# A convolution's output projection, half of its contraction by seven products and joined to the input projection's loop

## The chip, the core and the metric

The kernel runs on one core of a Trainium2 chip. The metric is the device time of one execution in microseconds (us). A core has five engines with queues of their own: TensorE (PE in the profile; its weight loads are PEld), VectorE (DVE), ScalarE (ACT), GpSimd (POOL) and SyncE (SP), which here only issues DMA transfers. Each engine works through its instructions in a fixed order, and an instruction that waits for a semaphore holds up everything behind it on that engine.

## The reference, cut to what matters

Two layers follow each other, a gated short convolution and a dilated windowed attention, on `x` of 1024 tokens and 1024 channels in float32. The change is in the first layer's end:

```python
h = rms_norm(x, conv_norm)                 # 1024 x 1024
b, c, u, z = split(h @ w_in, 4)            # w_in 1024 x 8192, each part 1024 x 2048
conv = sum(w_conv[k] * shifted(c * u, k) for k in range(3))
y = b * conv * silu(z)                     # 1024 x 2048
x = x + y @ w_out                          # w_out 2048 x 1024: the output projection
h = rms_norm(x, attn_norm)                 # and then the attention layer:
proj = h @ w_in                            # its q, k, v and z projections
```

The normalisation of the second layer needs, for every token, the mean square of the new `x` over all channels.

## The kernel before, in words

Everything is held transposed: channels on the 128 partitions, tokens along the free axis, the 1024 tokens as two halves (`hf` 0 and 1) of 512. A product of two float32 matrices is made from three products of rounded parts: each operand is split into a high and a low part (`split_w` for weights, lines 159 and 160, one ACT and one DVE instruction of 128x512 each; the same pair at lines 532 and 533, or 535 and 536, for activations), and `high*high`, `high*low` and `low*high` are added up in one PSUM bank. `product` (line 296) is the unit: a 512-deep contraction, four 128-deep slices with three matmuls of 128x128 by 128x512 each, so 12 matmuls.

The convolution's input projection and the attention's projection (called the QKV loop here) run in `strassen` (line 314): a pair of output tiles by two token halves and two halves of the contraction would be eight such units; a seven-product scheme makes it with seven, from added and subtracted operands. GpSimd mixes the weights (`mix`, line 274, four instructions a pair), ACT and DVE split them one pair ahead into eight buffers `ws`. The products are numbered 1, 2, 6, 5, 7, 4, 3; 4 and 3 of a pair run inside the next pair. `between(n, at)` hangs other work behind the product at place `at` of pair `n`.

In the input projection the gated result is multiplied together on DVE and GpSimd and stored to DRAM (`ydc`, 16 channel tiles by two halves, line 362). Then comes the output projection: for each token half and each of the eight output tiles `dt`, `chunk` adds four units (q = 0 to 3, 2048 deep) in one bank, plain; `row` adds `x`, stores the new tile to DRAM (`x1d`), splits and scales it into the operand blocks of the QKV loop (`B`, `T`), squares it on ACT and adds the square on GpSimd into `sqacc`. The weights of the output projection are loaded and split once for each half.

From `sqacc` come the statistics. `stats(hf)` sums it over partitions with four small matmuls (line 91) into the one bank of the pool `cst`, and DVE makes the inverse root of it in small instructions on 128x4 elements (lines 97 and 63 to 67, tile `rtok`). `spread(hf, rtok)` transposes `rtok` on PE (line 105) into the same bank, ACT copies it; `spread(hf, ms2)` does the same for the mean squares, and DVE turns them (lines 111, 112). For half 0 all three stand between the rows of half 1 in the output projection, and for half 1 in pair 1 of the QKV loop, at places 0, 5 and 6.

TensorE's order is the program's order (`manual_schedule`). On the other engines a scheduler sets it when the kernel is built. Tiles `f` (12 buffers of 128x512) serve nearly every intermediate. The blocks `blka` to `blkg` and `xb` hold split operands of 512 x 512.

## Time and profile before

| | |
|---|---|
| runs | 1918.7, 1921.18 and 1921.12 us, median 1921.12 |
| the profiled execution | 1914.92 us, of which the span from its first to its last instruction is 1913.1 us |
| busy share of the span | PE 98%, DVE 77%, POOL 48%, ACT 46% |
| input projection | 0 to 636 us of the span |
| output projection | 636 to 812.5 us |
| QKV loop, then attention | from 812.5 us |

The busy time of PE is a modelled one, since matmuls are pipelined: one shows as 0.39 us and the next starts 0.227 us after it. What matters is where PE has nothing to do, and what ends that wait. In the rows of a timeline, the brackets give how long the engine had been idle and who released it.

### The profile page before, as it was taken

Reading aid. Unit: us, or ns where it says so; the run is one execution under the profiler, and the core shown is the slowest. Engines: PE = TensorE matmul, PEld = TensorE weight load, DVE = VectorE, ACT = ScalarE, POOL = GpSimd, SP = SyncE. Lnnn points to the kernel's source line nnn. Section 1 sums busy time; section 2 is a strip of 40 time slices with the busy share of each in tenths; the row PEclk is TensorE's granted clock in tenths of the full one; section 3 lists DMA queues with packets and bytes.
Section 4 is the critical chain, followed back from the end, with each engine's and each line's share of the span. In section 5 each row is a group of like instructions: output and inputs, shape, how many; then the busy total and the mean of one; then the engine's idle time right before and its main releaser. Section 6 shows DMA issues by size and latency. Waiting matters only on the chain. (4 is left out here: it accounts for less than half of the span.)

```text
span 1913.1 us, 30523 instructions
## 1 busy us (share of the span) xinstructions
PE 1881.6 (98%) x10850; PEld 1544.4 (81%) x10850; DVE 1466.4 (77%) x2780; ACT 887.4 (46%) x2037; POOL 911.4 (48%) x841
## 2 busy tenths in 40 slices
PE   8999999999999999999999999999999999989999
PEld 6888888888888788888888888888888886777877
DVE  7966666666656746598988798878888787988886
ACT  6533333333333535454434443433443437978880
POOL 1376666766666211244545554555454562433340
PEclk9999999999999999999999999999999999999999
DMA  6222223222322656423323332433232437896842
GB/s 217 84 81 90 89 76 107 88 88 76 96 83 83 231 164 228 155 94 124 112 89 129 111 115 84 133 107 114 78 132 88 132 123 252 268 303 214 254 130 89
DMA packets 117801, 253.79 MB, mean 133 GB/s; under 512 B 18494, under 2 KB 23838, under 8 KB 117648
## 3 DMA queue, kind: packets, MB, share of 16 engines
q1 hardware_dynamic: 93280, 176.89, 28.4%
q0 software_dynamic: 24368, 74.95, 12.0%
q8 instruction: 85, 1.39, 0.3%
q14 instruction: 68, 0.56, 0.1%
HBM read 192.53 MB, written 67.64 MB: 136 GB/s over the span
## 5 line engine op out<-in xcount | busy, mean ns | idle before, releaser
L160 DVE TENSOR_TENSOR ws<-wr,ws 128x512 fp32r<-128x512 f32 x283 | 287.1, 1017 | 121.1 <-ACT ws L159 119.3
L159 ACT ACTIVATE ws<-wr 128x512 fp32r<-128x512 f32 x283 | 178.0, 630 | 365.2 <-PE pp L302 239.2
L159 ACT ACTIVATE ws<-sr 128x512 fp32r<-128x512 f32 x276 | 173.3, 631 | 342.1 <-PE pp L302 277.7
L274 POOL TENSOR_TENSOR sr<-wr 128x512 f32<-128x512 f32 x138 | 197.5, 1431 | 247.6 <-DMA wr<-in_conv_w_in 106.5
L160 DVE TENSOR_TENSOR ws<-sr,ws 128x512 fp32r<-128x512 f32 x276 | 230.7, 842 | 82.6 <-ACT ws L159 80.4
L311 DVE TENSOR_TENSOR f<-pp,f 128x512 f32<-128x512 f32 x207 | 141.6, 684 | 86.4 <-PE pp L302 79.0
L961 ACT ACTIVATE xs<-xs,nl 128x256 f32<-128x256 f32 (+2 forms) x384 | 160.9, 427 | 0.2 <-DVE nl L955 0.2
L307 ACT ACTIVATE f<-pp 128x512 f32<-128x512 f32 x231 | 134.2, 581 | 6.5 <-PE pp L302 6.5
L274 POOL TENSOR_TENSOR sr<-wr,sr 128x512 f32<-128x512 f32 x69 | 90.5, 1311 | 67.7 <-issue 55.2
L955 DVE CUSTOM_DVE_ANT_0 xs<-ps,bt 128x256 f32<-128x256 f32 (+2 forms) x384 | 102.5, 326 | 19.9 <-PE pt L968 12.2
L299 PE MATMUL pp<-blkf,ws 128*128 128x512 f32 x276 | 109.9, 398 | 0.7 <-ACT f L307 0.7
L299 PE MATMUL pp<-blka,ws 128*128 128x512 f32 x276 | 107.5, 390 | 0.7 <-ACT f L307 0.7
L301 PE MATMUL pp<-blkd,ws 128*128 128x512 f32 x276 | 107.9, 391 | 0.0
L299 PE MATMUL pp<-blkb,ws 128*128 128x512 f32 x276 | 107.8, 390 | 0.0
L299 PE MATMUL pp<-blkd,ws 128*128 128x512 f32 x276 | 107.6, 390 | 0.0
L302 PE MATMUL pp<-blke,ws 128*128 128x512 f32 x276 | 107.6, 390 | 0.0
L299 PE MATMUL pp<-blkg,ws 128*128 128x512 f32 x276 | 107.6, 390 | 0.0
L299 PE MATMUL pp<-blke,ws 128*128 128x512 f32 x276 | 107.5, 390 | 0.0
L302 PE MATMUL pp<-blkf,ws 128*128 128x512 f32 x276 | 107.5, 389 | 0.0
L302 PE MATMUL pp<-blkb,ws 128*128 128x512 f32 x276 | 107.5, 389 | 0.0
L301 PE MATMUL pp<-blkg,ws 128*128 128x512 f32 x276 | 107.4, 389 | 0.0
L301 PE MATMUL pp<-blke,ws 128*128 128x512 f32 x276 | 107.4, 389 | 0.0
(336 smaller groups left out, 5165.9 us busy)
## 6 DMA issues: line engine op xcount, KB each, us to landing
wr<-in_conv_w_in SPq DMA_DIRECT2D x128, 256.0 KB, 3.1
wr<-in_wqk SPq DMA_DIRECT2D x96, 256.0 KB, 3.4
qkd<-blkc POOLq DMA_DIRECT2D x48, 512.0 KB, 4.3
qk<-qkd SPq DMA_DIRECT2D x48, 512.0 KB, 5.2
wr<-in_conv_w_out SPq DMA_DIRECT2D x64, 256.0 KB, 3.2
f<-in_x SPq DMA_DIRECT2D x48, 256.0 KB, 4.1
wr<-in_wv SPq DMA_DIRECT2D x48, 256.0 KB, 3.1
vd<-blkc POOLq DMA_DIRECT2D x96, 128.0 KB, 2.7
```

The source lines that it names most:

```text
L159: nc.scalar.activation(t[:, 0], src, AF.Copy)
L160: nc.vector.tensor_tensor(t[:, 1], src, t[:, 0].bitcast(F32), op=OP.subtract)
L274: nc.gpsimd.tensor_tensor(t, x, y, op=op)
L299: nc.tensor.matmul(ps, w[:, 0, ws], b[:, k, 0], start=new and k == 0, stop=False, skip_group_check=not new)
L301: nc.tensor.matmul(ps, w[:, 0, ws], b[:, k, 1], start=False, stop=False, skip_group_check=not new)
L302: nc.tensor.matmul(ps, w[:, 1, ws], b[:, k, 0], start=False, stop=end and k == 3, skip_group_check=not new)
L307: nc.scalar.activation(t, ps, AF.Copy)
L311: nc.vector.tensor_tensor(m, ps, m, op=OP.add)
L955: nc.vector.tensor_tensor_reduce(out=x, in0=flat[s][:, cols], in1=u["bt"][s][:, bs], op0=OP.add, op1=OP.min, scale=-1.0, scalar=3e38, accu ...
L961: nc.scalar.activation(x, x, AF.Exp, bias=nm, scale=-1.0, accum_out=L)
```

## The change

The first half of the output projection's contraction (channel tiles 0 to 7 of `y`) is moved into the input projection's `strassen` call, as four more pairs (`out_pair`; pair i makes output tiles i and i+4 for both halves). The first of the four is plain, with eight units named a to h (`prepare(..., plain=True)`); the other three use the seven products. The mixed operands for them are made by `y_mix` on GpSimd in four places of the input projection, from tiles that are loaded back, and are stored to a new DRAM tensor `ymd`; `y_block` loads and splits them, at the places in `moves`. `put` adds `x` and stores the partial result to `x1d`. The second half of the contraction (tiles 8 to 15) stays plain, two units a tile, in the order tile i and i+4 of half 0, then of half 1; each `row` loads the partial result from `x1d` in place of `x`. Its weights are loaded and split once for both halves, and products 4 and 3 of the last pair run between its first units. `row` keeps the four tiles that it reloaded before (`kept`). The statistics of half 0 move into pairs 0 and 1 of the QKV loop (places 3 and 6 of pair 0, place 0 of pair 1), and those of half 1 start one place later (place 1 of pair 1).

```diff
+    ymd = dram.tile([5, 4, P, HALF], F32, name="ymd")
...
-        def prepare(s1_, s2_):
+        def prepare(s1_, s2_, plain=False):
 
             w = {}
             r1, r2 = raw_w(s1_, 2), raw_w(s2_, 2)
             lo_, up_ = slice(0, HALF), slice(HALF, 1024)
+            if plain:
+                for dt, r in enumerate((r1, r2)):
+                    for kh, cs in enumerate((lo_, up_)):
+                        w[dt, kh] = split_w(r[:, cs])
+                        yield w
+                return
...
-        def strassen(sources, pair, between, made):
+        def strassen(sources, pair, between, made, after=lambda: iter(())):
 
             w = [list(prepare(*sources[0]))[-1]]
             made()
-            last = None
+            last = {}
             for n in range(len(sources)):
                 now = pair(n, w[n])
-                nxt = prepare(*sources[n + 1]) if n + 1 < len(sources) else iter(())
-                for at, (name, who) in enumerate(((1, now), (2, now), (4, last), (6, now), (5, now), (3, last), (7, now))):
-                    if who is not None:
+                nxt = prepare(*sources[n + 1]) if n + 1 < len(sources) else after()
+                order = ((1, now), (2, now), (4, last), (6, now), (5, now), (3, last), (7, now)) if 1 in now else (
+                    ("a", now), (4, last), ("b", now), (3, last), ("c", now), ("d", now), ("e", now), ("f", now),
+                    ("g", now), ("h", now))
+                for at, (name, who) in enumerate(order):
+                    if name in who:
                         who[name]()
                     between(n, at)
                     got = next(nxt, None)
                     if got is not None and len(w) == n + 1:
                         w.append(got)
                 last = now
-            last[4]()
-            last[3]()
+            return last
+
+        Y, WO = {}, {}
...
+        def load_y(hf, q):
+            Y[hf, q] = block("abgc"[2 * hf + q])
+            for i in range(4):
+                y = ftile()
+                nc.sync.dma_start(y, ydc[hf, 8 + 4 * q + i])
+                nc.scalar.activation(Y[hf, q][:, i, 0], y, AF.Copy)
+                nc.vector.tensor_tensor(Y[hf, q][:, i, 1], y, Y[hf, q][:, i, 0].bitcast(F32), op=OP.subtract)
+
+        def out_w(dt):
+            r = raw_w(a["conv_w_out"][dt, 1], 2)
+            for c in range(2):
+                yield split_w(r[:, c * HALF:c * HALF + HALF])
...
+            NI = len(pairs)
+            YB, YT = {}, {}
+
+            def y_block(which, slot, i, src):
+                d = YT if isinstance(which, int) else YB
+                if i == 0:
+                    d[which] = block(slot)
+                t = ftile()
+                nc.sync.dma_start(t, src)
+                nc.scalar.activation(d[which][:, i, 0], t, AF.Copy)
+                nc.vector.tensor_tensor(d[which][:, i, 1], t, d[which][:, i, 0].bitcast(F32), op=OP.subtract)
+
+            def y_part(kh, hf, slot):
+                for i in range(4):
+                    y_block((kh, hf), slot, i, ydc[hf, 4 * kh + i])
+
+            def y_mixed(n, slot):
+                for i in range(4):
+                    y_block(n, slot, i, ymd[n, i])
+
+            def y_mix(i):
+                a11, a12, a22, a21 = (ftile() for _ in range(4))
+                for t, hf, e in ((a11, 0, i), (a12, 1, i), (a22, 1, i + 4), (a21, 0, i + 4)):
+                    nc.sync.dma_start(t, ydc[hf, e])
+                for n, (t, x, y) in enumerate(((a12, a12, a11), (a22, a22, a12), (a11, a22, a11), (a21, a21, a22))):
+                    nc.gpsimd.tensor_tensor(t, x, y, op=OP.subtract)
+                    nc.gpsimd.dma_start(ymd[n + 1, i], t)
+
+            def out_pair(n, w):
+                dts = (n - NI, n - NI + 4)
+                v = {}
+
+                def x_tile(c, hf):
+                    t = v["t", c, hf] = ftile()
+                    nc.sync.dma_start(t, a["x"][hf, dts[c]])
+
+                def put(c, hf, t, ps=None):
+                    x = v["t", c, hf]
+                    if ps is None:
+                        nc.gpsimd.tensor_tensor(t, t, x, op=OP.add)
+                    else:
+                        t = x
+                        nc.vector.tensor_tensor(t, ps, t, op=OP.add)
+                    nc.gpsimd.dma_start(x1d[dts[c], :, half(hf)], t)
+
+                def plain(c, hf, kh):
+                    if kh == 0:
+                        v[c, hf] = (cps if c else pp).tile([P, HALF], F32, name="pp", tag="pp")
+                        x_tile(c, hf)
+                    product(v[c, hf], w[c, kh], YB[kh, hf], kh == 0, kh == 1, False)
+                    if kh == 1:
+                        put(c, hf, None, v[c, hf])
+
+                if n == NI:
+                    return {name: lambda x=x: plain(*x) for name, x in zip("abcdefgh", (
+                        (0, 0, 0), (0, 0, 1), (1, 0, 0), (1, 0, 1), (0, 1, 0), (1, 1, 0), (0, 1, 1), (1, 1, 1)))}
...
+                def p7():
+                    product(v["x"], w[7], YT[3], False, True)
+                    put(1, 1, added(v["z"], copied(v["x"])))
+                    x_tile(1, 0)
+
+                def p4():
+                    product(v["x"], w[4], YT[4], False, True)
+                    put(1, 0, None, v["x"])
+                    x_tile(0, 1)
...
+            moves = {(NI - 1, 0): lambda: y_part(0, 0, "a"), (NI - 1, 1): lambda: y_part(1, 0, "b"),
+                     (NI, 1): lambda: y_part(0, 1, "f"), (NI, 2): lambda: y_part(1, 1, "d"),
+                     (NI, 3): lambda: y_mixed(2, "g"), (NI, 4): lambda: y_mixed(1, "c"),
+                     (NI, 5): lambda: y_mixed(3, "e"), (NI, 7): lambda: y_mixed(4, "f"),
+                     (NI + 3, 0): lambda: load_y(0, 0), (NI + 3, 1): lambda: load_y(0, 1),
+                     (NI + 3, 3): lambda: load_y(1, 0), (NI + 3, 4): lambda: load_y(1, 1)}
+
             def between(n, at):
+                if (n, at) in moves:
+                    moves[n, at]()
+                if n >= NI:
+                    return
                 e, pr = pairs[n]
+                if pr and not at and 6 <= e < 10:
+                    y_mix(e - 6)
...
+            def first_out():
+                for dt in (0, 4):
+                    for w in out_w(dt):
+                        WO.setdefault(dt, []).append(w)
+                        yield None
+
+            last_out = strassen([[a["conv_w_in"][e, 2 * pr + i] for i in range(2)] for e, pr in pairs] +
+                                [[a["conv_w_out"][i, 0], a["conv_w_out"][i + 4, 0], i == 0] for i in range(4)],
+                                pair, between, lambda: next(mix), first_out)
...
-                xt = ftile()
-                nc.sync.dma_start(xt, a["x"][hf, dt])
-                x1 = xt
-                nc.vector.tensor_tensor(x1, ps[dt], xt, op=OP.add)
+                cs, i = half(hf), dt % 4
+                x1 = ftile()
+                nc.sync.dma_start(x1, x1d[dt, :, cs])
+                nc.vector.tensor_tensor(x1, ps[dt, hf], x1, op=OP.add)
                 nc.gpsimd.dma_start(x1d[dt, :, cs], x1)
-                i = dt % 4
                 if hf == 0:
                     if i == 0:
                         B[dt // 4, 0] = block("ef"[dt // 4])
                     parts_of(B[dt // 4, 0], i, x1, g2[:, dt:dt + 1])
+                    if dt < 4:
+                        kept[i] = x1
...
-                    if hf == 1 and n == 2:
-                        stats(0, cst, sm)
-                    elif hf == 1 and n == 3:
-                        spread(0, rtok, cst)
-                    elif hf == 1 and n == 4:
-                        spread(0, ms2, cst)
-
+            chunk(0, 0, 0)
+            last_out[4]()
+            chunk(0, 0, 1)
+            last_out[3]()
+            for i in range(4):
+                for hf in range(2):
+                    for dt in (i, i + 4):
+                        for q in range(2) if (dt, hf) != (0, 0) else ():
+                            chunk(hf, dt, q)
+                        row(hf, dt)
+                    if hf == 0 and i < 3:
+                        for dt in (i + 1, i + 5):
+                            WO[dt] = list(out_w(dt))
...
-                if n == 1 and at == 0:
-                    stats(1, cst, sm)
-                elif n == 1 and at == 5:
-                    spread(1, rtok, cst)
-                elif n == 1 and at == 6:
-                    spread(1, ms2, cst)
+                if (n, at) in ((0, 3), (1, 1)):
+                    stats(n, cst, sm)
+                elif (n, at) in ((0, 6), (1, 5)):
+                    spread(n, rtok, cst)
+                elif (n, at) in ((1, 0), (1, 6)):
+                    spread(at // 6, ms2, cst)
```

Three places show how the instructions move. The first is GpSimd in the input projection, at a pair that has `y_mix` in it (line 274 before and 281 now are the weights' mixes, 496 and 497 now are `y_mix`). Before:

```order
L274 TENSOR_TENSOR sr<-wr 128x512
L465 TENSOR_TENSOR f<-f,R 128x512
L347 TENSOR_TENSOR f<-f,R 128x512
L274 TENSOR_TENSOR sr<-wr,sr 128x512
L263 DMA sk_86<-vecd 128x4x384
L492 TENSOR_TENSOR f<-f,sqacc 128x512
```

and now:

```order
L281 TENSOR_TENSOR sr<-wr 128x512
L496 TENSOR_TENSOR f<-f 128x512
L584 TENSOR_TENSOR f<-f,R 128x512
L497 DMA ymd<-f 128x512
L496 TENSOR_TENSOR f<-f 128x512
L372 TENSOR_TENSOR f<-f,R 128x512
L497 DMA ymd<-f 128x512
L496 TENSOR_TENSOR f<-f 128x512 x2
L281 TENSOR_TENSOR sr<-wr,sr 128x512
L264 DMA sk_86<-vecd 128x4x384
L497 DMA ymd<-f 128x512
L611 TENSOR_TENSOR f<-f,sqacc 128x512
```

Four subtractions and their stores stand between the third and the fourth mix of the weights, and behind the fourth.

The second is PE at the end of pair 0 of the QKV loop (`blkg` is the operand of product 7, `blke` that of product 1 of the next pair). Now:

```order
L309 MATMUL pp<-blkg,ws 128x512
L310 MATMUL pp<-blkg,ws 128x512
L105 MATMUL st<-ident,rtok 128x128 x4
L307 MATMUL pp<-blke,ws 128x512
L309 MATMUL pp<-blke,ws 128x512
```

The transposes of `rtok` for half 0 stand right behind product 7 of pair 0, where no small instruction stood; two products (6 is ahead of the statistics, 5 and 7 behind them) lie between the statistics' matmuls and these.

The third is DVE in pair 0 of the QKV loop, the last part of the inverse root for half 0 (line 914 is `fourth`, 670 and 673 split operands, 161 the weights, 319 the sum behind a product, here behind product 7). Before, in the output projection, with line 533 for the operands and 160 for the weights:

```order
L67 SCALAR_TENSOR_TENSOR rtok<-rtt,rtok 128x4
L533 TENSOR_TENSOR blkd<-f,blkd 128x512
L65 TENSOR_TENSOR rtt<-rtok 128x4
L160 TENSOR_TENSOR ws<-wr,ws 128x512
L66 SCALAR_TENSOR_TENSOR rtt<-rtt,ms_80 128x4
L67 SCALAR_TENSOR_TENSOR rtok<-rtt,rtok 128x4
```

and now:

```order
L161 TENSOR_TENSOR ws<-sr,ws 128x512
L66 SCALAR_TENSOR_TENSOR rtt<-rtt,ms_80 128x4
L670 TENSOR_TENSOR blka<-f,blka 128x512
L673 SCALAR_TENSOR_TENSOR blkb<-f,attn_norm,blkb 128x512
L670 TENSOR_TENSOR blka<-f,blka 128x512
L67 SCALAR_TENSOR_TENSOR rtok<-rtt,rtok 128x4
L161 TENSOR_TENSOR ws<-wr,ws 128x512
L319 TENSOR_TENSOR f<-pp,f 128x512
L65 TENSOR_TENSOR rtt<-rtok 128x4
L66 SCALAR_TENSOR_TENSOR rtt<-rtt,ms_80 128x4
L67 SCALAR_TENSOR_TENSOR rtok<-rtt,rtok 128x4
```

From line 97 to the last line 67 there are now 13 instructions of 128x512 among the small ones, where in the output projection there were three, and the last step of the root stands behind the sum of product 7.

94 lines of the change are left out of this document (36 added, 58 removed).

## The prediction

> **What bounds the kernel now.** I read the page's busy shares first, then the table of busy time by stage, then who waited for whom on PE.
>
> ```profile
> PE 1881.6 (98%) x10850; PEld 1544.4 (81%) x10850; DVE 1466.4 (77%) x2780; ACT 887.4 (46%) x2037; POOL 911.4 (48%) x841
> ...
> core 0: us, PE busy (x) PEld busy (x) DVE busy (x) ACT busy (x) POOL busy (x), PEclk, DMA share, GB/s
> 278.00:316.00 38.00, 38.00 (x169) 31.51 (x168) 24.17 (x29) 14.16 (x24) 25.88 (x21) 1.00 0.28 91
> 620.00:660.00 40.00, 39.07 (x171) 31.73 (x170) 32.90 (x45) 22.10 (x39) 13.28 (x11) 1.00 0.70 237
> 660.00:800.00 140.00, 140.00 (x627) 116.04 (x626) 73.91 (x113) 58.27 (x96) 26.23 (x27) 1.00 0.57 188
> 812.50:850.00 37.50, 37.33 (x172) 30.44 (x171) 35.72 (x52) 21.73 (x38) 14.15 (x10) 1.00 0.35 111
> ...
> PE pp L564 <- DVE blkb L533: 0.2, 1, 0.2
> PE st L105 <- DVE rtok L67: 0.2, 1, 0.2
> ```
>
> PE has no gap in the input projection or the output projection, beyond 0.93 us where the two meet (620 to 660). So the change is worth what it takes from PE's count, less every wait that it gives PE. The last stretch matters most: at the entry of the QKV loop DVE is busy 35.72 of 37.5 us, and PE waits there only 0.17.
>
> **What is removed.** A unit of 12 matmuls, from the first with `blka` to the first with `blkb`, and the wait where the input projection's last product 4 follows product 7:
>
> ```profile
> 591.45 0.39 PE L299 MATMUL pp<-blka,ws 128*128 128x512 f32 x1
> ...
> 594.17 0.39 PE L299 MATMUL pp<-blkb,ws 128*128 128x512 f32 x1
> ...
> 630.38 0.50 PE L299 MATMUL pp<-blkf,ws 128*128 128x512 f32 x1 [0.69 <-ACT f L307]
> ```
>
> A unit takes 594.17 - 591.45 = 2.72 us, 0.227 a matmul, not the 0.39 of a row. The output projection had 64 units. Now the first half of the contraction has 8 + 3x7 = 29, the second 32: three fewer, 36 matmuls, **-8.2 us**. In the 0.69 us product 4 waited for ACT to copy the bank after product 7. Unit a now stands between them, so this wait goes, and so does the 0.2 of line 564 (the first operands are now loaded a pair earlier): **-0.9**.
>
> **What is added at no cost.** Tiles of `y` to convert (one ACT and one DVE instruction each) go from 32 to 48, 24 of them in the last input pair and the plain pair, 17 units or 46 us. The stretch 620 to 660 had 16 in 40 us and kept PE fed with DVE at 32.9. The first operand of the seven-product pairs (`blkg`) is free after the third product of the plain pair's ten and wanted nine units, 24 us, later. Without that cover each late tile would cost 0.7 us. Transfers issued by SP: 32 fewer of output weights, 16 + 16 more of `y`, 8 more of `x1d`, so 8 more in all; none stands ahead of weights that PE wants within a pair. GpSimd issues 16 `ymd` stores and 16 more `x1d` stores, and has 9 more additions and 12 more mixes in pairs that no longer have gates. The 16 subtractions of `y_mix` are another matter:
>
> ```profile
> L274 POOL TENSOR_TENSOR sr<-wr 128x512 f32<-128x512 f32 x138 | 197.5, 1431 | 247.6 <-DMA wr<-in_conv_w_in 106.5
> L159 ACT ACTIVATE ws<-sr 128x512 fp32r<-128x512 f32 x276 | 173.3, 631 | 342.1 <-PE pp L302 277.7
> ...
> 301.34 0.57 POOL L362 DMA_DIRECT2D ydc<-g  x1 [0.30 <-POOL g L361]
> ```
>
> A step of two pairs is 38 us, and GpSimd works 25.88 of them. Four subtractions of 1.43 and four stores of 0.57 make 33.9: still under 38. The split of mixed weights waits for PE to free a buffer (277.7 of its idle time), not for GpSimd; with eight buffers, weights are ready at least five units (13.6 us) ahead, more than the 8.0 us that a step adds. I take **0**; bounds 0 and what the third rival says.
>
> **What is moved: the statistics of half 0.** This is the dear part. In the output projection the three steps were four units (10.9 us) apart and DVE half idle (73.91 of 140). Now they stand in pair 0 of the QKV loop. How long the same chain takes in a crowded DVE queue shows in pair 1 before, for half 1:
>
> ```profile
> 829.01 0.95 PE L91 MATMUL st<-ones,sqacc 128*128 128x1 f32 x8
> 829.82 0.49 PE L299 MATMUL pp<-blkf,ws 128*128 128x512 f32 x1
> ...
> 833.70 0.15 DVE L97 TENSOR_SCALAR ms<-st 128x4 f32<-128x4 f32 x1
> 834.40 0.13 DVE L63 TENSOR_SCALAR rtok<-ms 128x4 int32<-128x4 int32 x1
> 836.12 1.25 DVE L65 TENSOR_TENSOR rtt<-rtok 128x4 f32<-128x4 f32 x1
> 843.73 0.12 DVE L67 SCALAR_TENSOR_TENSOR rtok<-rtt,rtok 128x4 f32<-128x4 f32 x1
> ...
> 843.99 0.62 PE L105 MATMUL st<-ident,rtok 128*128 128x128 f32 x4 [0.17 <-DVE rtok L67]
> ```
>
> From the statistics' matmuls to the transposes, 15.0 us passed, and PE had six products to do between: just enough. Half 0 now gets the 0.81 us of the statistics and two products, 5 and 7, so 6.25 us. Were the chain as long, PE would wait **8.7**. The order gives a floor: the last step of the root stands on DVE behind the sum of product 7, so after product 7 come a split on ACT (0.63), the copy (0.58), the sum (0.69) and three small steps (0.45): **2.4**. To choose between, I work out DVE's queue.
>
> ```profile
> 812.51 0.39 PE L299 MATMUL pp<-blke,ws 128*128 128x512 f32 x1
> 820.05 0.39 PE L299 MATMUL pp<-xb,ws 128*128 128x512 f32 x1
> ...
> 812.71 0.69 DVE L573 TENSOR_TENSOR f<-pp,f 128x512 f32<-128x512 f32 x1 [1.30 <-PE pp L565]
> 813.98 1.81 DVE L591 SCALAR_TENSOR_TENSOR f<-f,attn_norm 128x512 f32<-128x512 f32 x1
> 817.42 1.78 DVE L533 TENSOR_TENSOR xb<-f,xb 128x512 fp32r<-128x512 f32 x1
> 822.93 0.71 DVE L684 TRANSPOSE_TENSOR_REDUCE st<-f 128x16 f32<-128x512 f32 x1
> 827.51 0.74 DVE L819 SCALAR_TENSOR_TENSOR f<-f,attn_norm 128x512 f32<-128x512 f32 x1
> ...
> 813.96 1.29 POOL L274 TENSOR_TENSOR sr<-wr 128x512 f32<-128x512 f32 x1 [7.77 <-DMA wr<-in_wqk]
> ```
>
> Before, ten instructions from the last row's sum (812.71) to the first reduction (end 823.64) took 10.9 us; now eleven stand ahead of the chain, some 11.5 us from the loop's start, while the statistics' matmuls end at 8.2 + 0.5 (below) + 0.95 = 9.6. So DVE comes 1.9 us late. The chain has 13 instructions of 128x512 at 0.65 and 12 small ones at 0.15: 10.3 us. The wait is 0.95 + 1.9 + 10.3 - 6.25 = **+6.9**. What is late next: behind this wait PE has all the rest, nothing hides it. By the rows, a DVE instruction that meets a GpSimd mix takes 1.81 instead of 0.74; I put no further such meeting into the 10.3.
>
> [...]
>
> Two smaller waits. `xb` was complete at 819.20, and the last three matmuls of product 6 want it at 820.05, 0.85 spare. Two more DVE instructions (1.3) now stand ahead of it: **+0.5** (0 to 1.5, if they also meet mixes). And the statistics of half 1, one product behind the turning of half 0's mean squares, want the one bank of `cst` back; DVE has two `blkb` splits ahead of line 111, and their tiles were late before:
>
> ```profile
> 832.87 1.38 SPq L551 DMA_DIRECT2D f<-x1d  x3
> 837.26 0.72 ACT L535 ACTIVATE blkb<-f,attn_norm 128x512 fp32r<-128x512 f32 x1 [3.00 <-DMA f<-x1d]
> ```
>
> That is 4.4 us from issue, behind two weight loads released by the split ahead of product 7's sum. Counted from that split: loads 1.0, tile 4.4, two splits on ACT and DVE 2.0, turning 0.7, so 8.1 us; PE wants the bank 1.2 (to the end of the root) + 0.6 + 2.72 + 0.6 + 2.72 = 7.8 after it. With 0.4 for semaphores: **+0.7** (0 to 2).
>
> **Sum.** -8.2 - 0.9 + 6.9 + 0.5 + 0.7 = **-1.0 us**, on a profiled execution of 1914.92 (span 1913.1). The median of the runs is 1921.12, 6.2 above that execution; I carry the difference over: 1920.1.
>
> **Rivals.** First, **DVE keeps up**: the wait is near its floor of 2.4, the small two vanish: -9.1 + 2.4 = -6.7, 1914.4. For it: 0.65 is an average in which meetings with mixes are included, and GpSimd may do its mixes earlier. Against it: DVE was over 5 us behind PE in this very place before. Second, **the wait is the full 8.7 and PE's clock falls behind it**. At the start, after 6 us without work, PE ran slow:
>
> ```profile
> 6.17 0.79 PE L384 MATMUL pp<-blka,ws 128*128 128x512 f32 x1 [6.17 <-ACT ws L159]
> 11.49 0.63 PE L386 MATMUL pp<-blka,ws 128*128 128x512 f32 x1
> 11.92 0.63 PE L384 MATMUL pp<-blka,ws 128*128 128x512 f32 x1
> 12.94 0.39 PE L384 MATMUL pp<-blka,ws 128*128 128x512 f32 x1
> ```
>
> One matmul each 0.43 us until 12.35: 6.2 us at about half rate, 3.1 lost. Then -9.1 + 8.7 + 3.1 + 1.2 = +3.9, 1925.0, slower. It decides from a wait of about 8.5 us on. Against it: no other gap in the trace is as long (2.9 at most), so a fall inside the kernel isn't seen. [...] Third, **GpSimd is the bound in the four steps**: if all its 12.1 us of waits in a step stay beside the added 8.0, a step is 8.0 late, and 4x8.0 less the 13.6 of lead is +18, 1938. It decides above 3.4 us late a step; the waits would have to be for PE, and most are for weights that SP loads early. That the change doesn't do what it says is excluded by PE's order, which has 36 matmuls fewer.
>
> **How the numbers follow.** My forecast 0.55, first rival 0.27, second 0.13, third 0.05. A change under 0.2%, 3.8 us, can't be told from none: the forecast is "same" (its own range 1917.3 to 1924), the first rival faster, the others slower. The range holds the first two and the second rival with both ends of the small waits: 1914.3 to 1926.5.
>
> **What would show it.** Right: PE's matmuls 36 fewer, no gap above 0.5 us before the last row of the output projection, one gap of 5 to 8 us ahead of line 105 in pair 0, released by `rtok` on DVE, and a small one ahead of line 91 in pair 1. Wrong: a gap there under 3 us, gaps in the four steps with `y_mix` or in the first seven-product pair, released by DVE or ACT on `ws` or `blk`, or matmuls 0.43 us apart behind the long gap.

## The result, and the profile after

The changed kernel takes 1935.42 us (median of 4 runs, 1934.92 to 1936.98) against 1920.65 us of the kernel before (4 runs, 1918.7 to 1921.18): 1.008 times as long, with a 95% interval of 1.0063 to 1.0098. The forecast was 1920.1, range 1914.3 to 1926.5. The busy shares and the waits on PE from its page and its list of waits (in total, how often, the longest, in us):

```profile
PE 1883.5 (97%) x10814; PEld 1541.6 (80%) x10814; DVE 1518.0 (78%) x2789; ACT 884.8 (46%) x2039; POOL 978.2 (51%) x910
...
PE pp L307 <- ACT f L315: 13.2, 11, 2.1
...
PE st L105 <- DVE rtok L67: 6.1, 1, 6.1
...
PE pp L309 <- DVE xb L670: 0.8, 1, 0.8
```

PE issued 36 matmuls fewer, as foreseen, and waited in places where it had not waited before. The largest sum, 13.2 us, is a wait for a copy on ACT that the prediction named only as one to be removed. Where the time went is read by following the same instruction in both timelines (start in us):

```profile
606.64 0.39 PE L307 MATMUL pp<-blkb,ws 128*128 128x512 f32 x1
...
818.15 0.39 PE L307 MATMUL pp<-blke,ws 128*128 128x512 f32 x1
...
875.91 0.39 PE L307 MATMUL pp<-blkd,ws 128*128 128x512 f32 x1
...
1606.77 0.40 PE L1037 MATMUL ps<-qk 64*64 64x128 f32 x2 [2.04 <-DVE ps L967]
```

and before, of the two that the prediction did not show:

```profile
858.90 0.39 PE L299 MATMUL pp<-blkd,ws 128*128 128x512 f32 x1
...
1589.80 0.40 PE L940 MATMUL ps<-qk 64*64 64x128 f32 x2 [2.04 <-DVE ps L870]
```

| the same instruction | before | after | behind by |
|---|---|---|---|
| product 2 in the last pair of the input projection | 594.17 | 606.64 | 12.5 |
| first product of the QKV loop | 812.51 | 818.15 | 5.6 |
| product 5 of pair 2 of the QKV loop | 858.90 | 875.91 | 17.0 |
| attention's first scores behind a wait of 2.04 | 1589.80 | 1606.77 | 17.0 |

So the input projection lost 12.5 us, the output projection won 6.8, the first two pairs of the QKV loop lost 11.4, and nothing changed from there to the attention. The attention itself lasts 323 to 331 us in the profiles of this study, without an order that follows the kernels' edits. That is why the experiments below are read by the start of these scores ("the attention's start": 1589.8 before, 1606.8 after), and by medians over runs where they were timed.

**The input projection.** One of the four steps with `y_mix` (two pairs), the busy time by engine (columns as in the prediction), after and then the same two pairs before:

```profile
306.70:348.32 41.62, 38.67 (x169) 31.38 (x168) 33.98 (x30) 13.81 (x24) 33.00 (x29) 1.00 0.39 133
```

```profile
305.86:343.94 38.08, 38.08 (x170) 31.55 (x169) 24.52 (x28) 14.16 (x24) 25.93 (x21) 1.00 0.29 91
```

GpSimd works 33.0 us in a step, near the 33.9 of the prediction, but the step is 41.6 us long in place of 38.1. GpSimd is idle for 8.6 of it, so it isn't the bound; what it does first is. The timeline of one such step after, the rows of the chain alone:

```profile
320.00 1.74 POOL L496 TENSOR_TENSOR f<-f 128x512 f32<-128x512 f32 x1
321.71 1.72 POOL L584 TENSOR_TENSOR f<-f,R 128x512 f32<-128x512 f32 x1
323.46 0.63 ACT L371 ACTIVATE f<-f 128x512 f32<-128x512 f32 x1 [4.46 <-POOL f L584]
324.00 0.58 ACT L315 ACTIVATE f<-pp 128x512 f32<-128x512 f32 x1
...
324.63 0.50 PE L307 MATMUL pp<-blke,ws 128*128 128x512 f32 x1 [1.45 <-ACT f L315]
325.13 5.00 DVE L161 TENSOR_TENSOR ws<-sr,ws 128x512 fp32r<-128x512 f32 x1 [2.84 <-ACT ws L160]
...
330.21 1.30 POOL L281 TENSOR_TENSOR sr<-wr,sr 128x512 f32<-128x512 f32 x1 [0.64 <-DVE ws L161]
...
331.54 4.00 SPq L155 DMA_DIRECT2D wr<-in_conv_w_in  x4
...
340.91 1.67 POOL L281 TENSOR_TENSOR sr<-wr 128x512 f32<-128x512 f32 x1 [2.48 <-DVE g L385]
...
344.30 0.63 ACT L160 ACTIVATE ws<-sr 128x512 fp32r<-128x512 f32 x1 [4.68 <-POOL sr L281]
344.84 0.58 ACT L315 ACTIVATE f<-pp 128x512 f32<-128x512 f32 x1
...
345.47 0.50 PE L307 MATMUL pp<-blke,ws 128*128 128x512 f32 x1 [1.50 <-ACT f L315]
...
382.58 1.78 POOL L281 TENSOR_TENSOR sr<-wr 128x512 f32<-128x512 f32 x1 [2.38 <-DMA wr<-in_conv_w_in]
```

and the rows before that answer to the copy, the fourth mix and the loads behind it:

```profile
318.92 0.58 ACT L307 ACTIVATE f<-pp 128x512 f32<-128x512 f32 x1
...
321.60 1.29 POOL L274 TENSOR_TENSOR sr<-wr,sr 128x512 f32<-128x512 f32 x1 [1.29 <-issue]
...
322.92 0.80 SPq L154 DMA_DIRECT2D wr<-in_conv_w_in  x2
```

Product 7 (`blke`) writes into the bank of product 6, so it waits until ACT has copied that bank (`u2`, line 315). Two ways lead from a subtraction to that copy. In a pair with `y_mix` it stands ahead of the gate's multiplication (line 584); ACT waits 4.46 us for this with its next activation, and the copy stands behind that one. And all four stand ahead of the fourth mix, the last reader of a raw weight tile: it starts at 330.21, before at 321.60, and the next weights are asked for at 331.54, before at 322.92. So the next pair's first mix is late (its releaser is named as a DVE instruction here and as the weights' transfer in the next step, last row), ACT waits 4.68 us for its result, and again the copy stands behind. In the first of the four pairs with `y_mix` of the changed kernel the weights were not yet that late, and PE did not wait:

```profile
283.04 0.58 ACT L315 ACTIVATE f<-pp 128x512 f32<-128x512 f32 x1
284.18 0.39 PE L307 MATMUL pp<-blke,ws 128*128 128x512 f32 x1
```

The copy there ends 0.56 us ahead of product 7 (in the profile before 2.7), so the first way alone used up most of the cover and not all. From the next pair on the late weights make a wait, and in the pairs with `y_mix` both ways add up; a step of two pairs then has two waits. Each costs 0.3 more than its row says (from 320.30, where the product ahead starts, to 327.49, where the one behind ends, are 7.19 us, where two products take 5.44: 1.75, by the row 1.45), so eight waits with 10.0 us make the 12.4.

**The output projection.** In the first seven-product pair product 6 (`blkg`) writes into the bank of product 1, whose copy is late:

```profile
664.77 0.63 ACT L371 ACTIVATE f<-f 128x512 f32<-128x512 f32 x1 [3.22 <-POOL f L615]
...
674.37 0.63 ACT L480 ACTIVATE blkf<-f 128x512 fp32r<-128x512 f32 x1 [2.71 <-DMA f<-ymd]
...
676.27 0.58 ACT L315 ACTIVATE f<-pp 128x512 f32<-128x512 f32 x1
...
676.89 0.50 PE L307 MATMUL pp<-blkg,ws 128*128 128x512 f32 x1 [2.06 <-ACT f L315]
```

ACT had waited 3.22 us for the last gate's multiplication on GpSimd and 2.71 for loads of mixed operands, and came to the copy behind them. This stage holds the gain of the 36 matmuls, and 1.9 us of small matmuls left it with the statistics.

**The QKV loop.** PE waits 6.11 us for the inverse root, as foreseen, and then runs slow (one matmul each 0.43 us, by the rows below, in place of 0.227). First and last row of the chain, and matmuls behind it:

```profile
827.81 0.95 PE L91 MATMUL st<-ones,sqacc 128*128 128x1 f32 x8
...
840.15 0.16 DVE L67 SCALAR_TENSOR_TENSOR rtok<-rtt,rtok 128x4 f32<-128x4 f32 x1
...
840.46 1.08 PE L105 MATMUL st<-ident,rtok 128*128 128x128 f32 x4 [6.11 <-DVE rtok L67]
...
842.62 0.63 PE L307 MATMUL pp<-blke,ws 128*128 128x512 f32 x1
843.05 0.63 PE L309 MATMUL pp<-blke,ws 128*128 128x512 f32 x1
```

### The profile page after: what moved, and what is told of

Same layout as the page of the kernel before. It is cut to its first block, busy times and chain, and to the rows that moved or that the text cites. A ratio compares the mean times of both kernels' runs of the same rounds, so it can differ in the third digit from the quotient of the medians.

```text
span 1934.9 us, 30577 instructions
## 1 busy us (share of the span) xinstructions
PE 1883.5 (97%) x10814; PEld 1541.6 (80%) x10814; DVE 1518.0 (78%) x2789; ACT 884.8 (46%) x2039; POOL 978.2 (51%) x910
## 5 line engine op out<-in xcount | busy, mean ns | idle before, releaser
L161 DVE TENSOR_TENSOR ws<-sr,ws 128x512 fp32r<-128x512 f32 x288 | 270.0, 943 | 95.8 <-ACT ws L160 93.9
L281 POOL TENSOR_TENSOR sr<-wr 128x512 f32<-128x512 f32 x144 | 209.4, 1454 | 245.9 <-DMA wr<-in_conv_w_in 96.5
L161 DVE TENSOR_TENSOR ws<-wr,ws 128x512 fp32r<-128x512 f32 x248 | 267.5, 1080 | 78.6 <-ACT ws L160 78.0
L160 ACT ACTIVATE ws<-wr 128x512 fp32r<-128x512 f32 x248 | 155.7, 629 | 290.6 <-PE pp L310 243.5
L307 PE MATMUL pp<-blka,ws 128*128 128x512 f32 x328 | 127.8, 390 | 0.7 <-ACT f L315 0.7
L307 PE MATMUL pp<-blkb,ws 128*128 128x512 f32 x328 | 128.0, 390 | 0.0
L310 PE MATMUL pp<-blkb,ws 128*128 128x512 f32 x328 | 127.6, 389 | 0.0
L309 PE MATMUL pp<-blka,ws 128*128 128x512 f32 x328 | 127.6, 389 | 0.0
L310 PE MATMUL pp<-blka,ws 128*128 128x512 f32 x328 | 127.6, 389 | 0.0
L309 PE MATMUL pp<-blkb,ws 128*128 128x512 f32 x328 | 127.6, 389 | 0.0
L307 PE MATMUL pp<-blkg,ws 128*128 128x512 f32 x320 | 125.2, 391 | 2.1 <-ACT f L315 2.1
L310 PE MATMUL pp<-blkg,ws 128*128 128x512 f32 x320 | 125.2, 391 | 0.0
L309 PE MATMUL pp<-blkg,ws 128*128 128x512 f32 x320 | 125.2, 391 | 0.0
L307 PE MATMUL pp<-blke,ws 128*128 128x512 f32 x288 | 113.9, 396 | 10.0 <-ACT f L315 10.0
L1052 DVE CUSTOM_DVE_ANT_0 xs<-ps,bt 128x256 f32<-128x256 f32 (+2 forms) x384 | 102.7, 326 | 20.4 <-PE pt L1065 11.8
L307 PE MATMUL pp<-blkf,ws 128*128 128x512 f32 x296 | 117.6, 397 | 0.5 <-ACT f L315 0.5
L309 PE MATMUL pp<-blkd,ws 128*128 128x512 f32 x296 | 115.6, 391 | 0.0
```

Of the source, the lines that this page charges most:

```text
L160: nc.scalar.activation(t[:, 0], src, AF.Copy)
L161: nc.vector.tensor_tensor(t[:, 1], src, t[:, 0].bitcast(F32), op=OP.subtract)
L281: nc.gpsimd.tensor_tensor(t, x, y, op=op)
L307: nc.tensor.matmul(ps, w[:, 0, ws], b[:, k, 0], start=new and k == 0, stop=False, skip_group_check=skip)
L309: nc.tensor.matmul(ps, w[:, 0, ws], b[:, k, 1], start=False, stop=False, skip_group_check=skip)
L310: nc.tensor.matmul(ps, w[:, 1, ws], b[:, k, 0], start=False, stop=end and k == 3, skip_group_check=skip)
```

## The experiments

### What makes the eight waits: the subtractions alone, in either kernel

Left out of the changed kernel:

```diff
-                    nc.gpsimd.tensor_tensor(t, x, y, op=OP.subtract)
                     nc.gpsimd.dma_start(ymd[n + 1, i], t)
```

> The changed kernel without the 16 subtractions of y_mix on GpSimd: the four loads and four stores of each place stay, the stored tiles are the loaded ones (so the mixed operands of three output pairs are wrong). The changed kernel takes 1935.4 and shows eight waits of PE, 0.3 to 1.7 us each, ahead of product 7 (released by the copy of u2 on ACT), which put it 12.4 us behind by 449 us of its span. Theory 'burst on GpSimd': the subtractions stand in GpSimd's queue ahead of the mixes and of the gate's multiplication for which ACT waits, and ACT's copy stands behind these; without them all eight waits go, 12.4 less, 1923.0. Rival 'loads and tiles': the four loads on SP's queue and the tiles held until their stores have landed make weights late; the eight waits stay, 1935, within 2. A third or so of the waits left (1927) would mean that GpSimd's four stores of 0.57 count too.

Measured: no wait of PE at all from 280 to 620 us of the span; product 2 of the last pair of the input projection starts at 594.7, 12.0 ahead of the changed kernel, and the attention at 1593.4, 13.4 ahead; 1921.4 us (one run). The loads, the stores and the tiles held by them cost nothing there: the subtractions do it.

Added alone to the kernel before, with the same function and the same four places:

> The kernel before with y_mix added in its four places (16 loads, 16 subtractions, 16 stores of a tensor that nothing reads). Theory 'burst on GpSimd': the eight waits ahead of product 7 come with it alone: 12.4 more, attention starts at 1602.2 (kernel before 1589.8), time 1932. Rival: they need something else of the change; under 4 us more, time 1924 or less.

Measured: six waits of 1.2 to 1.8 us, 8.9 in all; attention's start 1601.6, 11.8 behind the kernel before; 1931.3 us (one run). Nothing else of the change is needed. (Six waits for eight: the run with later statistics, further down, has six too, of 8.4 in all, with GpSimd, DVE and ACT in the same order there as in the changed kernel. So sums of waits differ between executions.)

### What about a subtraction costs: its number, its engine or its place

Six kernels do the same 16 subtractions elsewhere. First, on DVE in the same four places:

```diff
-                    nc.gpsimd.tensor_tensor(t, x, y, op=OP.subtract)
+                    nc.vector.tensor_tensor(t, x, y, op=OP.subtract)
```

> The changed kernel with the 16 subtractions of y_mix on DVE in place of GpSimd, the stores still issued by GpSimd. Theory 'burst on GpSimd': DVE works 24 of 38 us in these steps and takes 0.69 for a subtraction, 2.8 a step; the waits ahead of product 7 go, 1923.0, up to 1925. Rival: GpSimd's stores now wait for DVE and hold up the mixes behind them, and the subtractions stand ahead of splits in DVE's queue; waits of about 1 us in four to eight places are left, 1928 to 1934.

Measured: four waits, 5.7 us, and at two of them a stretch of 3.41 us at half clock (from 324.81 and from 406.73); product 2 of the last pair starts at 604.2, only 2.5 ahead of the changed kernel; attention's start 1601.9, 4.9 ahead, 1927.6 us (one run). The rival was nearer: in the input projection 10 of the 12.5 us stay, as waits and as slow clock.

Then one at a time on GpSimd, behind product 1 of 16 pairs in a row:

```diff
-                if pr and not at and 6 <= e < 10:
-                    y_mix(e - 6)
+                if not at and 0 <= 2 * e + pr - 13 < 16:
+                    y_mix(2 * e + pr - 13)
```

In this kernel and the next the second to fourth mixed operand are differences of the loaded tiles themselves and not of the differences made before; the work is the same.

> The changed kernel with y_mix cut into its 16 subtractions, one behind product 1 in each of 16 pairs in a row, each with two loads of its own and one store (16 loads more in all). Theory 'burst': what hurts is four subtractions and four stores at one place; one at a time (1.3 to 1.7 us and 0.57) fits into the 5.4 us that the copy of u2 has, and all waits ahead of product 7 go: 12.4 less, 1923.0, range 1922 to 1926. Rival 'sum': GpSimd has too much to do in a step whatever the order; the loss of some 3.1 us for each four subtractions stays and is only cut into smaller waits in 16 pairs: 1935, within 3. Rival 'loads and tiles': 32 loads where 16 were, worse: 1937 or more.

Measured: two waits, 2.0 us; attention's start 1596.9, 9.8 ahead of the changed kernel. 1929.75 us (10 runs from 1920.2 to 1935.6), 1.0047 of the kernel before (1.003 to 1.0064). The sum of work on GpSimd is the same and 16 loads came on top, so a bound by GpSimd's load is excluded. The theory's range of 1922 to 1926 was missed; at the attention's start 9.8 of its 12.4 us came.

The same behind product 6 of each pair, joined to two repairs that are told below:

> The changed kernel with three repairs: y_mix cut into 16 single subtractions, now behind product 6 of 16 pairs in a row (so behind the gate's multiplication in GpSimd's queue, not ahead of it); the statistics' places as in the run before with later statistics; and the mixed operands of products 7 and 4 converted later (behind product f of the plain pair and behind product 2 of the next pair). Theory: the three losses are separate and add up: 12.4 (waits ahead of product 7), 8.5 (wait for the inverse root and slow clock behind it), 4.1 (2.06 us wait in the first seven-product pair, its restart and the half-rate stretch behind it) come off 1935.4: 1910.4, range 1908 to 1914, some 9 below the kernel before. Attention then starts near 1581.8 us of the span, 25 ahead of the changed kernel (1606.8) and 8 ahead of the kernel before (1589.8). Rival: each repaired wait uncovers another (ACT and DVE are crowded where the projections meet); half of it comes back: 1918 to 1924, no gain over the kernel before.

Measured: twelve waits, 12.7 us, attention's start 1605.6; 1933.1 us, 1.0064 (1.0048 to 1.0081). The gain of the statistics is eaten: a place three products later turns two waits into twelve. GpSimd's rows in one such pair, and then the fourth mix in a pair of the run before:

```profile
483.68 1.74 POOL L497 TENSOR_TENSOR f<-f 128x512 f32<-128x512 f32 x1
485.71 0.57 POOL L498 DMA_DIRECT2D ymd<-f  x1 [0.30 <-POOL f L497]
486.30 1.31 POOL L281 TENSOR_TENSOR sr<-wr,sr 128x512 f32<-128x512 f32 x1
```

```profile
399.77 1.30 POOL L281 TENSOR_TENSOR sr<-wr,sr 128x512 f32<-128x512 f32 x1 [0.63 <-DVE ws L161]
```

Here the subtraction and its store stand right ahead of the fourth mix, which starts when they end; in the run before it still waited 0.63 for DVE, so the subtraction had not held it up.

Behind the fourth mix, two in each of eight pairs, at a place in the queue that was kept by hand:

> The changed kernel with y_mix in eight pairs, two subtractions each (24 loads, 16 stores; the tiles loaded half a pair earlier), and each kept in GpSimd's queue behind the fourth mix of the pair before and ahead of the first mix of its own pair, where the kernel before leaves GpSimd idle for 6 us. Theory 'raw weights': what costs is a subtraction ahead of the fourth mix, because that mix frees the raw weight tiles for the next loads; behind it the same 16 subtractions cost nothing: attention starts 12.4 ahead of the changed kernel (1606.8), at 1594.4 to 1595.5, time 1923. Rival 'burst': two subtractions and two stores in a row stand ahead of the next mixes in any case, and waits of about 1 us ahead of product 7 come in the eight pairs: 1599 or later, 1928 or more.

Measured: fourteen waits, 11.2 us, and attention's start 1613.5, later than in the changed kernel; 1944.7 us (one run). A kernel told further down has GpSimd, DVE and ACT in the same order up to 580 us of the span and shows five waits of 7.3 us there: so far apart are two executions of one order. In both, product 2 of the last pair starts later than in the changed kernel (612.7 and 607.3). The theory of the raw weights alone falls. What stood behind the subtraction now was another multiplication of GpSimd, for which DVE waits with the splits behind it in its queue (the rows are of DVE and GpSimd in one such pair):

```profile
329.53 2.34 DVE L620 TENSOR_TENSOR vb<-f 128x512 f32<-128x512 f32 x1 [2.44 <-POOL f L619]
...
339.39 1.29 POOL L281 TENSOR_TENSOR sr<-wr 128x512 f32<-128x512 f32 x1 [4.65 <-DMA wr<-in_conv_w_in]
```

Splits stand behind it on DVE, among them the last that reads a raw weight tile, and the next pair's first mix waits 4.65 us for its weights. I read that as the cause; no run shows it alone.

Last, single ones with the operands of the changed kernel and the other two losses repaired as far as known, once on DVE and once on GpSimd. On DVE they stand behind the sum of product 4 or 7, and GpSimd's stores behind the gate's multiplication:

> The changed kernel with: y_mix cut into 16 single subtractions, one in each of 16 pairs, on DVE, where they stand behind the sum of product 4 or 7, the stores behind the gate's multiplication in GpSimd's queue; the statistics' places as in the run with later statistics; and one of the eight blocks of y (for product 5) converted in the last pair of the input projection in place of the plain pair. Theory 'queue place': a subtraction costs nothing where nothing that feeds ACT or frees a raw weight stands behind it, DVE has 14 us free in a step and now gives 0.7 to 1.8 a pair; the losses of 12.4 and 8.5 go, and of the 4.9 in the output projection about half: attention starts at 1583 to 1586 (changed kernel 1606.8, kernel before 1589.8), time 1913 to 1917, faster than before by some 0.2 to 0.4%. Rival 'no slack': every added instruction of a step comes back as a wait, as in the runs with other places: attention at 1590 or later, 1920 or more, no gain.

> The same with the 16 single subtractions on GpSimd, behind product 1 of each pair as in the run with y_mix spread (two waits of 1.0 were left there), with their operands as in the changed kernel. Theory 'queue place': the subtractions stand between the third mix and the gate's multiplication, so two or more waits of about 1 us stay (2 to 6 us): attention starts at 1585 to 1590, time 1916 to 1921. Rival 'it is the engine's load': GpSimd at 30 of 38 us is the bound and all waits come back: attention at 1595 or later, 1926.

Measured from 280 to 620 us: on DVE two waits, 1.1 us; on GpSimd two, 2.5 us. So with the work of 16 subtractions unchanged the eight waits of 10.0 us nearly go on either engine, one at a time and at these places. Load is not the cause, place is (one at a time, two waits became twelve by the place alone; whether four at once would be harmless at a good place, no run shows); a simple rule for a harmless place ("behind the fourth mix") was tried and failed. The attention's start was 1591.5 and 1591.7, later than forecast: both keep a wait of 2.7 us in the output projection with a stretch at half clock, one of 0.7 and 0.6 ahead of it, and one of 1.7 and 1.0 at line 105, there for the statistics' bank. Times: 1918.28 us on DVE, 0.9997 of the kernel before (0.9984 to 1.001); 1925.67 on GpSimd, 1.0033 (1.0021 to 1.0045). That these two differ by 7 us with the same attention's start is not explained by anything ahead of the attention; the second time is that of the rival 'load', while the waits and the attention's start speak against it.

### The move of the statistics

Alone in the kernel before:

> The kernel before with nothing changed but the places of the statistics, which are put where the changed kernel has them (half 0 in pairs 0 and 1 of the attention's projection). Theory 'DVE is late': the price of the move does not depend on the rest of the change; PE waits about 6 us for the inverse root and 2.2 more go by the slow clock, 8.5 in all: attention starts at 1598.3 (kernel before 1589.8), time 1928. Rival 'row by row': the wait comes from the new order of the rows, which brings half 0 and half 1 to an end together; with the old rows it is under 3 us: attention starts below 1593, time 1922 or less.

Measured: a wait of 6.7 us at line 105, attention's start 1598.6, 8.8 behind the kernel before; 1931.4 us (one run). The price of the move doesn't depend on the new order of the rows.

Put further apart in the changed kernel, so that both halves' sums come early and their transposes five products later:

```diff
-                if (n, at) in ((0, 3), (1, 1)):
-                    stats(n, cst, sm)
-                elif (n, at) in ((0, 6), (1, 5)):
-                    spread(n, rtok, cst)
-                elif (n, at) in ((1, 0), (1, 6)):
+                if (n, at) in ((0, 3), (0, 6)):
+                    stats(at // 6, cst, sm)
+                elif (n, at) in ((1, 2), (1, 5)):
+                    spread(at // 5, rtok, cst)
+                elif (n, at) in ((1, 3), (1, 6)):
                     spread(at // 6, ms2, cst)
```

> The changed kernel with the statistics' places moved: sums of half 0 and half 1 behind products 6 and 7 of pair 0, the transposes of the inverse roots of half 0 and 1 behind product 4 and 3 of pair 1, those of the mean squares behind products 6 and 7 of pair 1. Theory 'DVE is late': the 6.11 us wait for the inverse root is the length of its chain in DVE's queue (11.4 us from the sums' end); five products (13.6 us) now lie between, so the wait goes, and the half-rate stretch behind it (2.2 us lost), 8.5 less: 1926.9, range 1925.5 to 1929. Rival 'one bank': six takings of the one statistics bank within eight products wait for each other; 3 us or more of waits are left: 1930 to 1935.

Measured: 0.35 us of waits at line 105 in place of 6.11; attention's start 1598.4, 8.4 ahead, of which 1.9 were there in the input projection already (the six waits for eight) and 6.5 come from the move; 1927.9 us, 1.0048 of the kernel before (1.0029 to 1.0067). DVE's chain was late by about what the prediction worked out, and more products between hide it; the one bank costs nothing like the rival's 3 us (in three of four later kernels with the same places 1.0 to 1.7). One stretch of 3.41 us at half clock is still there, now behind the wait for `xb` and the statistics' small matmuls.

### The wait where the projections meet

Two of the eight blocks of `y` converted later, and, in another kernel, three of them earlier, by other places in the table `moves`:

> The changed kernel with only the conversion of the mixed operands of products 7 and 4 put later. Theory 'queue on ACT': the 2.06 us wait in the first seven-product pair is ACT's copy of the bank standing behind conversions that wait for loads of ymd; with those loads asked for later the wait and the half-rate clock behind it go: 4.1 less, attention starts near 1602.7 in place of 1606.8, time 1931.3. Rival 'sum of conversions': ACT and DVE have too many conversions there in any order; a wait of 2 us shows up within the same pair or the next, attention starts within 1 us of 1606.8.

> The changed kernel with three of the eight blocks of y converted earlier (two in the last pair of the input projection, one behind the plain pair's first product), in place of all six behind the first in the plain pair. Theory 'sum of conversions': ACT and DVE have more conversions than fit between the plain pair's start and the first seven-product pair; spread over two pairs the 2.06 us wait, its restart, the slow clock behind it and the 0.49 us wait go: 4.9 less, attention starts near 1601.9 (changed kernel 1606.8), time 1930.5. Rival: it only moves to another product, as when two blocks were put later; attention starts within 1.5 us of 1606.8.

Measured: later, the wait moves from product 6 to product 7 and grows to 3.5 us; attention's start 1606.6, no gain (1932.0 us, one run). Earlier, it moves into the plain pair (1.8 us) with a second one of 1.25, and the wait for the root is 4.5 in place of 6.1; attention's start 1607.4, no gain (1938.5 us, one run). Neither place helps, so where the conversions stand is not shown to be the cause. The three repairs joined, with the subtractions behind the fourth mix:

> The three repairs together: subtractions behind the fourth mix, statistics' places as in the run with later statistics, blocks of y converted earlier. Theory: the three losses are separate: 12.4 + 8.5 + 4.9 = 25.8 off 1935.4 and off the start of attention (1606.8): attention starts at 1581 to 1583, 7 to 9 ahead of the kernel before (1589.8), time 1909.6, range 1908 to 1915, faster than before by about 0.5%. Rival: half of it comes back by waits that stood behind those: attention near 1590 or later, 1918 to 1924, no gain.

Measured: five waits, 7.3 us, in the input projection, 2.1 and 0.7 where the projections meet; attention's start 1600.7; 1931.5 us, 1.0065 (1.005 to 1.0081).

In the kernel with the subtractions on DVE the place shows the same chain as the four steps. GpSimd's part of its timeline:

```profile
652.55 4.67 POOL L616 TENSOR_TENSOR f<-f,R 128x512 f32<-128x512 f32 x1 [2.85 <-DVE f L319]
...
659.22 1.75 POOL L281 TENSOR_TENSOR sr<-wr,sr 128x512 f32<-128x512 f32 x1
...
668.87 2.13 POOL L281 TENSOR_TENSOR sr<-wr 128x512 f32<-128x512 f32 x1 [1.19 <-DMA wr<-in_conv_w_out]
```

The last gate's multiplication takes 4.67 us in place of 1.3, the fourth mix stands behind it, and the next weights come late. So this multiplication was put on DVE, and half 0's mean squares one place later:

```diff
-                        nc.gpsimd.tensor_tensor(c12, c12, R[:, half(1)], op=OP.mult)
+                        eng = nc.vector if e == NE - 1 else nc.gpsimd
+                        eng.tensor_tensor(c12, c12, R[:, half(1)], op=OP.mult)
```

> The kernel with 16 single subtractions on DVE, later statistics and one earlier block, and two more repairs: the last gate's multiplication (behind product 3 of the last input pair) on DVE in place of GpSimd, and the transposes of half 0's mean squares one place later. In the run before that multiplication took 4.67 us on GpSimd, under a row of DVE conversions, and the fourth mix behind it freed the raw weights late; the next pair's product 7 waited 2.70. Theory 'late raw weights': with it out of GpSimd's queue the weights come about 5 us earlier, the wait, its restart and the slow clock behind it go (4.7), and 1.7 of the wait for the statistics' bank: attention starts at 1585 to 1586.5 (1591.4 in that run, 1589.8 in the kernel before), time 1911.5 to 1914, 0.2 to 0.4% faster than the kernel before. Rival 'crowd': DVE's conversions take the place of the wait; attention starts within 1.5 of 1591.4, time 1918, no gain.

Measured: attention's start 1586.8, 4.7 earlier, somewhat later than forecast; 1916.11 us (12 runs from 1910.1 to 1921.1), 0.9978 of the kernel before, interval 0.9963 to 0.9993. It beats the kernel before by 0.2% and, by the two ratios, the changed one by 1.0%. The two edits were not run apart, but they act in different stages: from product 2 of the last pair to the QKV loop 209.6 us pass in place of 212.8, and its first two pairs take 49.2 in place of 51.2, without the wait of 1.7 for the bank. The wait is halved, not gone (GpSimd and PE in this kernel):

```profile
654.64 3.48 POOL L281 TENSOR_TENSOR sr<-wr,sr 128x512 f32<-128x512 f32 x1 [5.26 <-DVE ws L161]
...
672.25 0.50 PE L307 MATMUL pp<-blke,ws 128*128 128x512 f32 x1 [1.43 <-ACT f L315]
```

The fourth mix now waits 5.26 us for a split on DVE and takes 3.48: it ends 2.9 us earlier than in the run before, not 5. So in the output projection both theories hold in part: one late multiplication, and DVE's row of conversions, which takes its place.

## Why the prediction was wrong, point by point

Measured terms go by the waits, 0.3 added to each, and by what the stretches at half clock cost; behind the wait for the root that is 2.2 (from the transposes' start to the eleventh matmul behind them 4.97 us pass, before 2.77). They give the stages' differences back if the 1.9 us of small matmuls that went from the output projection to the QKV loop are counted (the kernel before with nothing but the statistics moved goes through the first in 216.4 in place of 218.3): 12.4 in the input projection, -8.2 - 1.5 + 4.8 - 1.9 = -6.8 in the output projection, 6.2 + 2.2 + 1.1 + 1.9 = 11.4 in the QKV loop.

| step of the prediction | predicted | measured |
|---|---|---|
| 36 matmuls less | -8.2 | -8.2 |
| waits of product 4 and at line 564 gone | -0.9 | -1.5 |
| `y_mix` | 0 | +12.4 |
| conversions of `y` | 0 | +4.8 |
| wait for the inverse root | +6.9 | +6.2 |
| clock behind it | 0 (in a rival) | +2.2 |
| `xb` | +0.5 | +1.1 |
| bank for the statistics of half 1 | +0.7 | 0 |
| sum | -1.0 | +17.0 |

The sum is that of the attention's start in the two profiles. The medians of the runs differ by 14.8; what takes 2.2 from it is not known, and the attention's own length varies by more.

**The step that failed is "The 16 subtractions of y_mix are another matter ... I take 0".** It compared GpSimd's work in a step (33.9) with the step's length (38), and gave the weights five units of lead from the eight buffers behind the split. The work was about right (33.0), and neither number decides. The lead is set further up, by two raw tiles that the fourth mix and the last split free; and the copy of `u2`, for which product 7 waits, stood on ACT behind instructions that wait for GpSimd. The copy had ended at 319.5 in the profile before, 2.7 us ahead of product 7 at 322.2: that was the whole cover. A subtraction takes 1.7 of it, and the mixes that begin late take the rest and more. The order shown ahead of the prediction had a subtraction ahead of the multiplication and all of them ahead of the fourth mix; the prediction read it for GpSimd's sum and not for who waits behind. The third rival had the place, with a chance of 0.05, but its cause (GpSimd as the bound) is excluded by the run with the work spread and the one on GpSimd with the changed kernel's operands, and its 18 us too.

**"What is added at no cost" failed too**, by 4.8 us: two waits of 2.06 and 0.49 with their restarts, and 1.7 by the clock. Its cause is shown in part only: a late multiplication on GpSimd is one piece of it, by the last run, and the rest stays open. DVE was named as the engine to watch (32.9 of 40 us), but the price was taken for a late tile of `y`, and what was late was again a copy on ACT and the raw weights.

**The wait for the inverse root was right**: 6.11 us for 6.9, by the chain as worked out (DVE ended it at 840.31, 12.5 us after the start of the statistics' matmuls; predicted 13.2. DVE came 1.0 us late where 1.9 was worked out, and the chain took 10.6 for 10.3). The run that moves the statistics in the kernel before has it at 6.7, the run that spaces them apart leaves 0.3. The second rival's clock was right in kind and wrong in its point: it decided from 8.5 us on, and the clock fell at 6.11 and cost 2.2. Nor does its counter-argument hold, that no fall is seen inside the kernel before: the attention in that profile has three (clock 0.50 from 1681.75, 1719.29 and 1838.76).

**The two small waits**: `xb` came 0.83 late (0.5 predicted), the bank never did (0.7). The 0.4 for semaphores in that 0.7 is shown by no run; from the root's last row on DVE to the first transpose on PE 0.15 us pass here (840.31 to 840.46).

**The rivals were taken as exclusive.** The clock fell and GpSimd's waits came in the same run, and both add to the wait that was forecast. A range from rivals that each change one term leaves out their sum. (Its upper end is not what it was worked out from, either: the second rival with 1.5 and 2.0 for the small waits gives 1927.3 and not 1926.5. Nothing hangs on it here.)

## What to carry to other kernels

Before an instruction is put at nothing because its engine has room, list what stands behind it in that queue, who waits for each, and how long each of those could wait; here 2.7 us of cover stood against 1.7 us for a subtraction and a first mix that came late, on an engine with 8.6 us idle. Follow a double buffer to its last reader, since an instruction ahead of that reader delays the next load (here four subtractions ahead of the fourth mix, which started at 330.21 in place of 321.60, and the loads at 331.54 in place of 322.92). And price rivals that can happen together as a sum.

## What the runs showed of the hardware

**In these profiles the stretches at half clock start on a raster of 3.413 us.** Busy time and granted clock (last but two) of the changed kernel in stretches of 3.41 us that follow each other from two edges of the slow stretches:

```profile
404.88:408.29 3.41, 1.73 (x9) 1.11 (x7) 1.05 (x1) 1.19 (x3) 3.39 (x4) 1.00 0.05 18
408.29:411.70 3.41, 3.41 (x15) 2.83 (x16) 2.93 (x1) 1.29 (x3) 3.40 (x4) 1.00 0.31 118
...
674.53:677.94 3.41, 1.35 (x7) 0.87 (x6) 3.41 (x7) 2.62 (x5) 0.54 (x1) 1.00 0.79 246
677.94:681.35 3.41, 3.41 (x10) 2.65 (x9) 2.42 (x5) 0.00 (x0) 2.10 (x3) 0.50 0.68 263
...
834.96:838.37 3.41, 0.00 (x0) 0.00 (x0) 3.41 (x7) 2.23 (x5) 0.00 (x0) 1.00 0.19 71
838.37:841.78 3.41, 1.32 (x6) 1.25 (x7) 2.59 (x8) 0.82 (x2) 0.00 (x0) 0.50 0.40 139
841.78:845.20 3.42, 3.42 (x10) 2.65 (x9) 0.25 (x1) 1.41 (x3) 2.35 (x2) 0.50 0.70 245
845.20:848.60 3.40, 3.40 (x18) 2.83 (x17) 3.39 (x6) 2.09 (x4) 0.91 (x2) 1.00 0.00 0
```

Behind the three stretches here with 0, 1.32 and 1.35 us busy the next one has a clock of 0.50; behind the one with 1.73 it has 1.00. In the run with two blocks converted later it has 0.52 behind one with 1.61 (363.25 to 366.66). The two slow stretches shown start 160.43 us apart, 47 times 3.413. The seven of the changed kernel up to 1900 us of its span all start on one such raster, within 0.01 us, and so do the three of the kernel before; the two in the run with `y_mix` on DVE, from 324.81 and 406.73, are 81.92 us apart, 24 times 3.413. The busy time of PE alone does not tell the next clock where small matmuls stand in a stretch: the statistics' matmuls are in one with 2.52 of the run with later statistics (823.10 to 826.50, clock 0.52 behind it) and in one with 2.52 of the changed kernel (824.72 to 828.13, clock 1.00 behind it), and in the attention of the changed kernel one is shown as busy throughout (1889.68 to 1893.09, all its matmuls write 128x64 or less) with 0.50 behind it. What a wait cost differed with where it fell. In the run without subtractions one of 2.82 us lay across an edge, 2.19 and 1.82 us busy on its two sides, and the clock stayed at 1.00 (its slow stretch from 824.47 is 47 times 3.413 behind the edge):

```profile
660.63:664.04 3.41, 2.19 (x10) 1.50 (x8) 3.41 (x7) 0.71 (x2) 0.00 (x0) 1.00 0.77 272
664.04:667.46 3.42, 1.82 (x8) 1.52 (x9) 3.42 (x7) 2.07 (x4) 1.04 (x2) 1.00 0.96 325
```

In the changed kernel one of 2.06 us lay within one stretch (674.53 to 677.94), and the next one's 3.41 us at a clock of 0.50 cost an estimated 1.7 more, half of its length.

**DVE and GpSimd instructions took longer in places where both engines worked.** A split on DVE took 5.00 us at 325.13 of the changed kernel, where three 128x512 instructions of GpSimd began within it (at 325.20 and, two in a row, at 327.02), and a multiplication on GpSimd took 4.67 at 652.55 of the kernel with the subtractions on DVE, where DVE had a row of conversions and splits (from 652.39 to 656.07); the shortest of their kind take 0.64 and 1.28. What in the meeting makes them long no run shows.
